# Loading the input a second time with channels on partitions, so that the first norm's units need no TensorE transposes, and reordering the first loads

## The chip, the cores and the metric

The kernel runs on one core of one Trainium2 chip. The metric is the device time of the whole kernel in microseconds (us), the median of several executions. TensorE (PE) does matrix products and transposes, VectorE (DVE) and ScalarE (ACT) elementwise work, GpSimd (POOL) a few small operations, and SyncE (SP) issues the loads.

## The reference

A two-layer decoder trunk over 256 tokens of 2048 channels, all float32. Only the start of layer 0 matters here:

```
def rms_norm(x, g):
    xf = x.astype(jnp.float32)
    y = xf * lax.rsqrt(jnp.mean(xf * xf, axis=-1, keepdims=True) + EPS)
    return (y * g.astype(jnp.float32)).astype(x.dtype)
...
    proj = hn @ w_in          # hn = rms_norm(h, even_norm), w_in: 2048 x 5392
    qa, ka, va, qkv_b, z, beta_raw, a_raw = jnp.split(proj, EVEN_SPLITS, axis=-1)
```

Behind it come a sliding-window attention and a gated delta rule, an output projection, a SwiGLU feed-forward layer, a second layer with a gated MLP mixer and another feed-forward layer, and a last norm.

## The kernel before, in words

Tokens are two tiles of 128 (t = 0, 1), channels four chunks of 512 (n = 0 to 3). A product needs its left operand with channels on partitions. That operand is a "unit": for one n and one t a tile of 128 channels x 4 x 128 tokens, in two parts, hi (rounded to the fast matmul format by ScalarE, the CAST rows) and lo (the rest, a VectorE subtraction). `fill_unit` makes it from token-major rows: four TensorE transposes into PSUM (`side<-ident,h` in the profile), a VectorE multiplication with the norm's gain (`unit<-side,gains`), then `split` for hi and lo. The other factor of the norm, one over the root mean square (`rstd`), is a number per token, and is put in only when a product's result is read from PSUM (`scale=self.rstd[t]`). It needs sums of squares: `chunk_stats` has ScalarE square each of the eight 128x512 pieces of the input (`junk<-h`) and add up; `end_norm` then has VectorE sum up and scale (`tot`, `rstda`) and GpSimd raise to the power -0.5 (`rstd<-rstda,mhalf`), once per token tile.

`dense` makes one product of 512 columns: it loads the weights in four pieces (`raw`, one for each n), splits each of a piece's four blocks into hi (`whi`, ScalarE) and lo (`wlo`, VectorE), and issues six matmuls a block: hi x hi, hi x lo and lo x hi for each token tile. The first product of the kernel is `kvg`, 272 columns wide (keys, values and gates; 96 matmuls of 128x272), the next `qa0` with 512 columns (`mm<-whi,unit ... 128x512`). `raw` has three buffers, `whi` and `wlo` six each. When kvg is done, ScalarE reads its results with `rstd` into `ba`, `unit` and `va`; the gates' small chain (`beta`, `ge`, `gg`) and the decay tables of the delta rule (`unit<-unit,gp` on VectorE, `unit<-gp,unit` on GpSimd, multiplied by `one`) run beside qa0.

The order on every engine is fixed when the kernel is built. All operations are recorded with a priority (`prio`, lower first; `schedule.early` is an earliest time in ns); a list scheduler (`plan`) with costs of its own then writes one order for all engines, and each engine keeps to it: an instruction that waits holds up all behind it. Eight completion counters are shared by SP's loads, so SP issues at most eight ahead of the oldest that has not landed.

Of the kernel before, what the change touches and what calls it, by code (L numbers as in the profile page):

```python
# [10 lines left out]
F32R = mybir.dt.float32r  # L11
BF16 = mybir.dt.bfloat16
AF = mybir.ActivationFunctionType
ALU = mybir.AluOpType
AX = mybir.AxisListType

P = 128
D = 2048
SEQ = 256
NT = SEQ // P  # L20
KB = 4
CW = 512
NCH = D // CW
# [33 lines left out]
def chunk_width(cols):  # L57
    return sum(b - a for a, b in cols)
# [256 lines left out]
class Trunk:  # L315
# [67 lines left out]

    def load_consts(self):
        nc, t = self.nc, self.t
        self.ident = self.keep((P, P), "ident")
        nc.sync.dma_start(self.ident, t["ident"])
        self.gains = self.const(t["gains"], [P, 4, 16], "gains")
        self.junk = self.keep((P, CW), "junk", BF16)
        self.mhalf = self.keep((P, 8), "mhalf")  # L390
        nc.vector.memset(self.mhalf, -0.5)
        self.phalf = self.keep((P, 8), "phalf")
        nc.vector.memset(self.phalf, 0.5)
# [57 lines left out]
    def fill_unit(self, srcs, gain=None):  # L451
# [10 lines left out]
            self.split(ps, unit[t])  # L462
        return unit


    def dense(self, w, units, off, width=CW, pcs=None, lag=0, first=False):

        nc = self.nc  # L470
        ps = [self.bank(width) for _ in range(NT)]
        pcs = range(len(units)) if pcs is None else pcs
        size = P * KB * width
        todo = deque()

        def product(t, x, k, hi, lo, st, sp):
            xh, xl = x[t]
            nc.tensor.matmul(ps[t], xh[:, k], hi, start=st, stop=False)
            nc.tensor.matmul(ps[t], xh[:, k], lo, start=False, stop=False)
            nc.tensor.matmul(ps[t], xl[:, k], hi, start=False, stop=sp)  # L480

        for unit, pc in zip(units, pcs):
            with self.prio(2 * pc - 19 if first else 0):
                raw = self.slot((P, KB, width), F32, "raw")
                o = off + pc * size
                nc.sync.dma_start(raw, w[o:o + size].rearrange("(p k n) -> p k n", p=P, k=KB))
            for k in range(KB):
                with self.prio(0):
                    tags = ("unit", "unit") if lag and k % 2 else ("whi", "wlo")
                    hi, lo = [self.slot((P, width), F32R, tag) for tag in tags]  # L490
                    nc.scalar.copy(hi, raw[:, k])
                    nc.vector.tensor_tensor(lo, raw[:, k], hi.bitcast(F32), ALU.subtract)
                with self.prio(9):
                    todo.append((unit, k, hi, lo, pc == pcs[0] and k == 0, pc == pcs[-1] and k == KB - 1))
                    product(0, *todo[-1])
                    if len(todo) > lag:
                        product(1, *todo.popleft())
        with self.prio(9):
            for x in todo:
                product(1, *x)  # L500
        return ps
# [376 lines left out]
    def even_mixer(self, gain):  # L878
        units = self.units
        off, mix, outs, c = 0, [], [], {}  # L880
        for name, cols in EVEN_CHUNKS:
            ps = self.dense(self.t["even_in"], units, off, chunk_width(cols), first=name == "kvg")
            off += D * chunk_width(cols)
            with self.prio(1):
                if name == "kvg":
                    self.end_norm()
                    ba, kk = self.gate_columns(ps), self.attn_kv(ps)
                else:
                    c[name] = self.zgate(ps) if name[0] == "z" else self.tok_tile(ps)
            if name == "kvg":  # L890
                self.schedule.early = 9000.0
                with self.prio(0):
                    self.load_tables()
                self.schedule.early = 0.0
                with self.prio(2):
                    self.gates(ba)
                    kT = self.attn_keys(kk)
            kind, i = name[:-1], int(name[-1]) if name[-1].isdigit() else 0
            with self.prio(2):
                if kind == "k":  # L900
                    keys = self.delta_k(i, c[name])
                elif kind == "q":
                    queries = self.delta_q(i, c[name])
                elif kind == "v":
                    outs.append(self.delta(i, keys, *queries, c[name]))
            with self.prio(3):
                if kind == "qa":
                    mix.append(self.new_unit())
                    for t in range(NT):
                        self.attention(i, t, c[name], mix[i][t], kT)  # L910
        w = self.t["even_out"]
        for n in range(NCH):
            self.residual(n, self.dense(w, mix, n * D * CW, pcs=range(0, 2)))
        with self.prio(1):
            rest = [self.delta_out(outs[i], c[f"z{i}"]) for i in range(2)]
        self.project(w, rest, gain, pcs=range(2, 4))
# [109 lines left out]
    def run(self):  # L1026
        g = lambda i: self.gains[:, i]
        with self.prio(-20):
            self.load_consts()
        self.begin_norm()  # L1030
        self.h = [[None] * NCH for _ in range(NT)]
        for n in range(NCH):
            with self.prio(2 * n - 20):
                self.load_hidden(n)
            with self.prio(1):
                self.units.append(self.fill_unit([self.h[t][n] for t in range(NT)], g(0)[:, KB * n:KB * (n + 1)]))
        with self.prio(1):
            for n in range(NCH):
                self.chunk_stats(n)
        self.even_mixer(g(1))  # L1040
        self.ffn(0, g(2))
        self.odd_mixer(g(3))
        self.ffn(1, None)
        with self.prio(1):
            self.finish()
# [10 lines left out]
def const_table():  # L1056
    import numpy as np

    c = np.zeros((P, NCONST, P), np.float32)
    j, i = np.meshgrid(np.arange(P), np.arange(P), indexing="ij")  # L1060
    same = (j // 64) == (i // 64)
    c[:, C_TRI] = same & (j <= i)
    c[:, C_TB] = np.where(i < 64, same & (j > i), -1.0 * (same & (j <= i)))
    c[:, C_SU] = j > i
    c[:, C_H0] = j < 64
    c[:, C_DMASK] = np.where(j <= i, 0.0, NEG)
    c[:, C_ONE] = 1.0
    c[:, C_AM] = np.where(i <= j, 0.0, NEG)
    c[:, C_AM + 1] = np.where(i > j, 0.0, NEG)
    for lv in range(2):  # L1070
        s = SB << lv
        c[:, C_LVL + lv] = (j // (2 * s) == i // (2 * s)) & ((j // s) % 2 == 0) & ((i // s) % 2 == 1)
    c[:, C_SAME] = j // SB == i // SB
    c[:, C_UP] = (j // SB == i // SB) & (j < i)
    c[:, C_DIAG] = (j % SB == i) & (i < SB)
    return c, (j == i).astype(np.float32), (j <= i).astype(np.float32)
# [14 lines left out]
def arrays_of(inputs):  # L1091
    import numpy as np

    i = {k: np.asarray(v) for k, v in inputs.items()}
    col = lambda v: v.reshape(-1, P).T
    ctab, ident, ltri = const_table()
    a = {
        "x": i["x"].reshape(NT, P, NCH, CW).transpose(0, 2, 1, 3),
        "ctab": ctab,
        "ident": ident,  # L1100
        "ltri": ltri,
        "gains": np.stack([col(i["even_norm"][0]), col(i["ffn_norm"][0]), col(i["odd_norm"][0]),
                           col(i["ffn_norm"][1])], axis=1),
        "conv": i["even_conv"][0].T.reshape(24, P, 4).transpose(1, 0, 2),
        "rows": np.concatenate([i["even_dt_bias"][0], i["even_a_log"][0], i["even_sinks"][0], i["even_onorm"][0]]),
        "bs": i["odd_b_s"][0].T,
        "ws": i["odd_w_s"][0].transpose(2, 0, 1),
        "lng": i["odd_ln_g"][0],
        "lnb": i["odd_ln_b"][0],
        "final_g": i["final_norm"],  # L1110
        "even_in": layout(i["even_w_in"][0], [c for _, c in EVEN_CHUNKS]),
        "even_out": layout(i["even_w_out"][0], PLAIN_CHUNKS),
        "odd_in": layout(i["odd_w_in"][0], ODD_CHUNKS),
        "odd_out": layout(i["odd_w_out"][0], PLAIN_CHUNKS),
    }
    for l in range(2):
        a[f"gate{l}"] = layout(i["ffn_w_gate"][l], FF_CHUNKS)
        a[f"up{l}"] = layout(i["ffn_w_up"][l], FF_CHUNKS)
        a[f"down{l}"] = layout(i["ffn_w_down"][l], PLAIN_CHUNKS)
    return {k: np.ascontiguousarray(v) for k, v in a.items()}  # L1120
# [22 lines left out]
```

## Time and profile before

| | |
|---|---|
| time, median of 3 runs (lowest, highest) | 2188.86 us (2186.94, 2188.88) |
| the profiled execution's own time | 2188.75 us |
| its span, first to last instruction | 2186.7 us |
| TensorE busy in the span | 2166.3 us (99%) |
| VectorE, ScalarE, GpSimd busy | 1326.0, 1138.5, 59.0 us |
| first matmul of kvg, first of qa0 | 10.88 us, about 26 us |

A row of the timeline gives start and length of a group of equal neighbours (xN), and in brackets how long its engine had stood idle and what ended that. Lengths are from start to full end; two neighbours overlap a little, so the distance from start to start is the smaller number.

### The profile page before, as it was taken

The page shows a single profiled execution, that of the slowest core. Times are in us where ns is not written, and L with a number is a line of the kernel's source. Part 1 is how long each engine was busy: PE and PEld are TensorE (multiplying, and loading weights), DVE is VectorE, ACT ScalarE, POOL GpSimd, SP SyncE. Part 2 cuts the span into 40 slices and gives each one's busy share as a digit, 9 for nine tenths or more (in the row PEclk, how much of TensorE's full clock was granted, in tenths as well). Part 3 has the DMA queues.
Part 4 walks back from the last instruction along what each step waited for, and adds up shares of the span by engine and source line. Part 5 has one row for each costly group of instructions (what it writes and reads, how often), then busy time and mean ns, then how long its engine had stood idle before and what let it go on. Part 6 is the DMA issues. An engine that isn't in the chain of part 4 may idle for free.

```text
span 2186.7 us, 27199 instructions
## 1 busy us (share of the span) xinstructions
PE 2166.3 (99%) x10044; PEld 1792.4 (82%) x10044; DVE 1326.0 (61%) x2265; ACT 1138.5 (52%) x2034; POOL 59.0 (3%) x68
## 2 busy tenths in 40 slices
PE   8999999999999999999999999999999999999998
PEld 7787888888888888888888888888888888888886
DVE  8796886765555555555555576665555555555553
ACT  7665654554545554444445545554555445444453
POOL 1010100000000000000010000000000000000000
PEclk9999999999999999999999999999999999999999
DMA  7342435555555555555565555555555555565553
GB/s 250 123 156 76 154 117 172 182 186 191 192 193 193 184 187 189 192 193 193 192 237 186 196 168 186 178 189 192 193 185 187 189 192 191 192 209 194 194 195 132
DMA packets 58453, 399.07 MB, mean 183 GB/s; under 512 B 6976, under 2 KB 7232, under 8 KB 11216
## 3 DMA queue, kind: packets, MB, share of 16 engines
q1 hardware_dynamic: 57168, 393.61, 53.0%
q0 software_dynamic: 1152, 3.74, 0.5%
q8 instruction: 78, 1.28, 0.2%
q14 instruction: 55, 0.45, 0.1%
HBM read 395.22 MB, written 2.10 MB: 182 GB/s over the span
## 4 chain that ended last, share of the span: by engine, by line
PE 96%; DVE 2%; ACT 1%; issue 1%; DMA 0%; POOL 0%; SPq 0%; POOLq 0%; DVEq 0%; ACTq 0%
PE mm L178 90%; PE side L178 6%; DVE unit L178 1%; DVE wlo L178 1%; ACT whi L178 0%; DMA h<-in_x 0%; ACT junk L178 0%; POOL unit L178 0%; DVE uc L178 0%; SPq L178 0%; DVE yt L178 0%; DVE h L178 0%; DVE yr L178 0%; ACT L178 0%; ACT unit L178 0%
## 5 line engine op out<-in xcount | busy, mean ns | idle before, releaser
L178 PE MATMUL mm<-whi,unit 128*128 128x512 f32 (+1 forms) x5864 | 1829.8, 391 | 0.0
L178 DVE TENSOR_TENSOR wlo<-raw,whi 128x512 fp32r<-128x512 f32 (+1 forms) x1466 | 1011.0, 691 | 806.0 <-ACT whi L178 800.7
L178 ACT CAST whi<-raw 128x512 fp32r<-128x512 f32 (+1 forms) x1466 | 909.1, 621 | 938.6 <-DVE wlo L178 752.6
L178 PEld LDWEIGHTS mm<-whi,unit 128*128 128x128 f32 x5864 | 1097.8, 188 | 226.0 <-issue 4.7
L178 PE MATMUL mm<-wlo,unit 128*128 128x512 f32 (+1 forms) x2932 | 1140.9, 390 | 0.0
L178 PEld LDWEIGHTS mm<-wlo,unit 128*128 128x128 f32 x2932 | 551.1, 188 | 110.8 <-issue 0.2
L178 PE MATMUL side<-unit,unit 128*128 128x128 f32 (+3 forms) x448 | 60.6, 285 | 0.0
L178 PEld LDWEIGHTS side<-unit,unit 128*128 128x128 f32 (+2 forms) x448 | 54.4, 182 | 5.6 <-issue 1.4
L178 ACT ACTIVATE unit<-mm,rstd 128x512 f32<-128x512 f32 (+1 forms) x84 | 56.1, 671 | 2.2
L178 PE MATMUL side<-ident,unit 128*128 128x128 f32 x356 | 55.0, 273 | 0.4 <-DVE unit L178 0.4
L178 PEld LDWEIGHTS side<-ident,unit 128*128 128x128 f32 x356 | 44.1, 140 | 12.2 <-issue 2.3
L178 DVE TENSOR_TENSOR unit<-side,unit 128x512 fp32r<-128x512 f32 (+1 forms) x64 | 43.6, 690 | 10.8 <-ACT unit L178 10.2
L178 ACT CAST unit<-side 128x512 fp32r<-128x512 f32 x60 | 35.1, 586 | 19.5 <-PE side L178 17.5
L178 DVE TENSOR_TENSOR unit<-unit,unit 128x512 fp32r<-128x512 f32 (+1 forms) x56 | 39.7, 714 | 1.0
L178 PE MATMUL mm<-unit,unit 128*128 128x512 f32 x132 | 35.9, 389 | 0.0
L178 ACT COPY unit<-side 128x512 f32<-128x512 f32 (+1 forms) x36 | 20.6, 585 | 25.4 <-PE side L178 25.4
L178 DVE SCALAR_TENSOR_TENSOR unit<-side,conv,unit 128x255 f32<-128x255 f32 (+2 forms) x72 | 31.1, 473 | 2.4 <-ACT unit L178 2.4
L178 ACT ACTIVATE junk<-h 128x512 bf16<-128x512 f32 x40 | 25.1, 628 | 11.1 <-DVE h L178 8.4
L178 DVE SCALAR_TENSOR_TENSOR unit<-mm,rstd,unit 128x512 f32<-128x512 f32 x44 | 30.9, 743 | 0.0
L178 DVE TENSOR_TENSOR h<-mm,h 128x512 f32<-128x512 f32 x40 | 25.8, 683 | 6.3 <-PE mm L178 6.3
L178 PEld LDWEIGHTS mm<-unit,unit 128*128 128x128 f32 x132 | 24.8, 188 | 5.1
L178 PE MATMUL side<-ident,h 128*128 128x128 f32 x128 | 20.7, 291 | 7.3 <-DMA h<-in_x 7.3
(119 smaller groups left out, 461.4 us busy)
## 6 DMA issues: line engine op xcount, KB each, us to landing
raw<-in_gate SPq DMA_DIRECT2D x88, 1024.0 KB, 4.8
raw<-in_up SPq DMA_DIRECT2D x88, 1024.0 KB, 4.8
raw<-in_down SPq DMA_DIRECT2D x88, 1024.0 KB, 4.9
raw<-in_even_in SPq DMA_DIRECT2D x40, 1024.0 KB, 4.9
raw<-in_odd_in SPq DMA_DIRECT2D x32, 1024.0 KB, 4.9
raw<-in_even_out SPq DMA_DIRECT2D x16, 1024.0 KB, 4.8
raw<-in_odd_out SPq DMA_DIRECT2D x16, 1024.0 KB, 4.9
raw<-in_even_in SPq DMA_DIRECT2D x4, 544.0 KB, 6.7
```

The source lines that it names most:

```text
L178: f(*map(real, args), **{k: real(a) for k, a in kw.items()})
```

## The change

The host passes the input in a second layout, `xt`: for each t and n the 128 x 4 x 128 block with channels on partitions. `first_unit` loads it straight into the buffer of a unit and multiplies with the gain in place; the transposes of the first norm are gone. The token-major input `x` is still loaded, for the sums of squares and the residual, but later and with its squares behind the units in the recorded order. The gains are asked for on ScalarE's own load queue, the identity matrix later. The first weights come second on SP's queue, ahead of the second input block.

```
-        self.ident = self.keep((P, P), "ident")
-        nc.sync.dma_start(self.ident, t["ident"])
-        self.gains = self.const(t["gains"], [P, 4, 16], "gains")
+        self.gains = self.keep((P, 4, 16), "gains")
+        nc.scalar.dma_start(self.gains, t["gains"])
+        with self.prio(-13):
+            self.ident = self.const(t["ident"], [P, P], "ident")
...
+    def first_unit(self, n, gain):
+
+        unit = []
+        for t in range(NT):
+            x = self.unit()
+            with self.prio(4 * n + 2 * t - 30):
+                self.nc.sync.dma_start(x, self.t["xt"][t, n])
+            with self.prio(1):
+                self.nc.vector.tensor_tensor(x, x, gain.unsqueeze(2).to_broadcast([P, KB, P]), ALU.mult)
+                unit.append([self.unit(F32R), self.unit(F32R)])
+                self.split(x, unit[t])
+        return unit
...
-            with self.prio(2 * pc - 19 if first else 0):
+            with self.prio(4 * pc - 29 if first else 0):
...
-                self.schedule.early = 9000.0
+                self.schedule.early = 12000.0
...
         for n in range(NCH):
-            with self.prio(2 * n - 20):
+            self.units.append(self.first_unit(n, g(0)[:, KB * n:KB * (n + 1)]))
+        for n in range(NCH):
+            self.schedule.early = 8500.0
+            with self.prio(-12):
                 self.load_hidden(n)
+            self.schedule.early = 0.0
             with self.prio(1):
-                self.units.append(self.fill_unit([self.h[t][n] for t in range(NT)], g(0)[:, KB * n:KB * (n + 1)]))
-        with self.prio(1):
-            for n in range(NCH):
                 self.chunk_stats(n)
...
+        "xt": i["x"].reshape(NT, P, NCH, KB, P).transpose(0, 2, 4, 3, 1),
```

What the scheduler makes of it is seen in the order of instructions. SP's queue at its head, before (`raw` are weights of kvg, `h` the input):

```order
L178 DMA ident_0_0_4484<-in_ident 128x128
L178 DMA gains_0_1_4486<-in_gains 128x64
L178 DMA h_0_4_4490<-in_x 128x512
L178 DMA h_0_5_4492<-in_x 128x512
L178 DMA raw_76_4494<-in_even_in 128x1088
L178 DMA h_0_20_4496<-in_x 128x512
L178 DMA h_0_21_4498<-in_x 128x512
```

and with the change, where `unit<-in_xt` is the input with channels on partitions:

```order
L178 DMA unit_4_4478<-in_xt 128x512
L178 DMA raw_52_4480<-in_even_in 128x1088
L178 DMA unit_8_4484<-in_xt 128x512
L178 DMA unit_12_4486<-in_xt 128x512
L178 DMA raw_85_4488<-in_even_in 128x1088
L178 DMA unit_16_4490<-in_xt 128x512
L178 DMA unit_20_4492<-in_xt 128x512
```

The first weights moved from fifth to second place; the eight `h` loads now stand behind the fourth piece of weights, and qa0's first weights (`raw_233`) behind those eight.

ScalarE around the end of kvg, before (`whi_200` and `unit_66` are the last casts of kvg, `whi_258` the first of qa0, `ba` reads kvg's result with `rstd`):

```order
L178 CAST whi_200_4750<-raw_175_4575 128x272
L178 CAST unit_59_4757<-unit_58_4726 128x512
L178 ACTIVATE ea_0_239_4765<-rows_0_229_4596 128x8
L178 CAST unit_66_4785<-unit_65_4754 128x512
L178 CAST whi_258_4805<-raw_257_4640 128x512
L178 CAST whi_266_4810<-raw_257_4640 128x512
L178 CAST whi_274_4817<-raw_257_4640 128x512
L178 CAST whi_282_4826<-raw_257_4640 128x512
L178 ACTIVATE ba_0_214_4834<-mm_79_4562,rstd_0_210_4789 128x2x8
```

and with the change, from kvg's last cast (`unit_34`) to qa0's first (`whi_234`):

```order
L178 CAST unit_34_4714<-unit_32_4500 128x512
L178 ACTIVATE junk_0_38_4680,ss_0_39_4684<-h_0_41_4553 128x512
L178 ACTIVATE junk_0_38_4680,ss_0_38_4679<-h_0_44_4558 128x512
L178 ACTIVATE junk_0_38_4680,ss_0_39_4684<-h_0_45_4560 128x512
L178 ACTIVATE junk_0_38_4680,ss_0_38_4679<-h_0_48_4563 128x512
L178 ACTIVATE junk_0_38_4680,ss_0_39_4684<-h_0_49_4567 128x512
L178 ACTIVATE ba_0_190_4767<-mm_55_4524,rstd_0_186_4759 128x2x8
L178 ACTIVATE unit_192_4769<-mm_55_4524,rstd_0_186_4759 128x2x64 x2
L178 ACTIVATE ba_0_190_4767<-mm_58_4539,rstd_0_189_4765 128x2x8
L178 ACTIVATE va_0_194_4773<-mm_55_4524,rstd_0_186_4759 128x128
L178 ACTIVATE unit_192_4769<-mm_58_4539,rstd_0_189_4765 128x2x64
L178 CAST whi_234_4776<-raw_233_4600 128x512
```

Before, the four casts of qa0's first weights stood ahead of the first instruction that needs `rstd`. Now five of the eight squares, and then six reads with `rstd` of both token tiles, stand between kvg's last cast and qa0's first.

VectorE at the end of kvg with the change (`unit_32` is multiplied with the gain here; then kvg's last weights, the last lo, and the sums for `rstd`):

```order
L178 TENSOR_TENSOR unit_31_4691<-unit_28_4498,unit_30_4663 128x512
L178 TENSOR_TENSOR unit_32_4500<-unit_32_4500,gains_0_0_4474 128x512
L178 TENSOR_TENSOR wlo_169_4710<-raw_151_4534,whi_168_4703 128x272
L178 TENSOR_TENSOR wlo_177_4717<-raw_151_4534,whi_176_4707 128x272
L178 TENSOR_TENSOR unit_35_4727<-unit_32_4500,unit_34_4714 128x512
L178 TENSOR_REDUCE tot_0_184_4753<-ss_0_38_4679 128x1
L178 TENSOR_SCALAR rstda_0_185_4757<-tot_0_184_4753 128x1
```

The last gain multiplication stands three instructions ahead of the last lo; before, the sums for `rstd` stood ahead of the last lo, and now behind it.

## Rows read from the trace of the kernel before

**Rows 1.** The page: span, and TensorE's busy time.

```profile
span 2186.7 us, 27199 instructions
...
PE 2166.3 (99%) x10044; PEld 1792.4 (82%) x10044; DVE 1326.0 (61%) x2265; ACT 1138.5 (52%) x2034; POOL 59.0 (3%) x68
```

**Rows 2.** Busy time by stretch: length, PE, PEld, DVE, ACT, POOL, clock, DMA.

```profile
10.80:26.00 15.20, 15.17 (x115) 14.94 (x114) 13.59 (x34) 12.82 (x35) 2.50 (x2) 1.00 1.02 373
```

**Rows 3.** Timeline of SP's queue: issue of kvg's first weights.

```profile
2.60 0.43 SPq L178 DMA_DIRECT2D raw<-in_even_in  x1
```

**Rows 4.** DMA issues at 1.6, 2.6 and 4.0 us: KB, us to landing.

```profile
h<-in_x SPq DMA_DIRECT2D x1, 256.0 KB, 2.8
...
raw<-in_even_in SPq DMA_DIRECT2D x1, 544.0 KB, 6.0
...
raw<-in_even_in SPq DMA_DIRECT2D x1, 544.0 KB, 7.2
```

**Rows 5.** VectorE by form, 0 to 23.2 us: count, busy, mean ns, idle before.

```profile
L178 DVE TENSOR_TENSOR wlo<-raw,whi 128x272 fp32r<-128x272 f32 x16 | 6.4, 436 | 1.5 <-ACT whi L178 1.4
L178 DVE TENSOR_TENSOR unit<-side,gains 128x512 f32<-128x512 f32 x8 | 5.4, 686 | 5.1 <-PE side L178 5.0
```

**Rows 6.** Timeline of VectorE in kvg.

```profile
9.08 1.50 DVE L178 TENSOR_TENSOR wlo<-raw,whi 128x272 fp32r<-128x272 f32 x4 [0.45 <-ACT whi L178]
10.50 1.47 DVE L178 TENSOR_TENSOR unit<-side,gains 128x512 f32<-128x512 f32 x2
...
15.82 1.28 DVE L178 TENSOR_TENSOR unit<-side,gains 128x512 f32<-128x512 f32 x2
```

**Rows 7.** Timeline of ScalarE, 4 to 32 us.

```profile
4.47 0.63 ACT L178 ACTIVATE junk<-h 128x512 bf16<-128x512 f32 x1 [2.45 <-DMA h<-in_x]
...
5.23 0.63 ACT L178 ACTIVATE junk<-h 128x512 bf16<-128x512 f32 x1
...
18.06 0.78 ACT L178 CAST whi<-raw 128x272 fp32r<-128x272 f32 x2
...
26.96 0.27 ACT L178 ACTIVATE ba<-mm,rstd 128x16 f32<-128x16 f32 x1 [0.48 <-POOL rstd L178]
...
27.88 2.19 ACT L178 CAST whi<-raw 128x512 fp32r<-128x512 f32 x4
...
31.84 1.28 ACT L178 ACT_TABLE_LOAD   x1
```

**Rows 8.** Timeline of GpSimd: the powers of the first norm and of another.

```profile
23.50 3.43 POOL L178 TENSOR_TENSOR rstd<-rstda,mhalf 128x1 f32<-128x1 f32 x2 [23.05 <-DVE rstda L178]
...
444.99 1.05 POOL L178 TENSOR_TENSOR rstd<-rstda,mhalf 128x1 f32<-128x1 f32 x1 [92.34 <-DVE tot L178]
447.57 0.56 POOL L178 TENSOR_TENSOR rstd<-rstda,mhalf 128x1 f32<-128x1 f32 x1 [1.53 <-DVE rstda L178]
```

**Rows 9.** Timeline of VectorE around those powers at 445 and 447.6 us.

```profile
444.94 0.69 DVE L178 TENSOR_TENSOR unit<-unit,unit 128x512 fp32r<-128x512 f32 x1
...
447.90 0.69 DVE L178 TENSOR_TENSOR wlo<-raw,whi 128x512 fp32r<-128x512 f32 x1 [0.41 <-ACT whi L178]
```

**Rows 10.** Timeline of TensorE's weight loads (PEld): two rows of transposes.

```profile
9.26 1.57 PEld L178 LDWEIGHTS side<-ident,h 128*128 128x128 f32 x8 [3.14 <-DMA h<-in_x]
...
13.32 0.48 PEld L178 LDWEIGHTS side<-ident,h 128*128 128x128 f32 x4
```

**Rows 11.** The chain that ended last: 45 matmuls of kvg in a row.

```profile
17.50 5.64 PE mm L178 x45
```

**Rows 12.** Timeline of TensorE: qa0's third matmul, a wait, the kernel's end.

```profile
26.50 0.39 PE L178 MATMUL mm<-wlo,unit 128*128 128x512 f32 x1
...
40.04 0.70 PE L178 MATMUL side<-unit,one 128*128 128x512 f32 x2 [1.25 <-DVE unit L178]
...
2176.93 0.84 PE L178 MATMUL mm<-unit,unit 128*128 128x512 f32 x3
```

**Rows 13.** Busy time by stretch at the end, columns as in rows 2.

```profile
2180.00:2181.00 1.00, 0.00 (x0) 0.00 (x0) 0.30 (x4) 0.05 (x1) 0.55 (x1) 0.75 0.00 0
```

## The prediction

> **What bounds the kernel now.** I read the page first: TensorE is busy 99% of a span of 2186.7 us [rows 1], so only about 20 us are idle, and an edit that adds no matmul work can give or take only what lies around waits. The busy time by stretch then shows where: nothing of kvg is multiplied before 10.8 us, and from 10.8 to 26.0 us TensorE is busy 15.17 of 15.20 us, VectorE 13.59, ScalarE 12.82 [rows 2]: three engines nearly full at once. The reader is to see that taking work from TensorE there does not by itself end kvg sooner. qa0's third matmul starts at 26.50 [rows 12]; with two of some 0.23 us ahead of it, qa0 starts at 26.05. That is the moment to compare: behind it TensorE works almost without a gap, so a shift of it reaches the end.
>
> **What goes.** 32 transposes. Sixteen ran before 10.8 us, in time that TensorE would have idled; the other sixteen cost 0.12 us each [rows 10], 1.9 us of the full stretch. VectorE's eight gain multiplications stay, 686 ns each [rows 5]. They read SBUF now instead of PSUM; the subtraction that reads SBUF alone takes 0.69 too [rows 9], so I take no change there.
>
> **When kvg can start.** The first `xt` block is 256 KB and SP's first load, at 0.74 us; an `h` block takes 2.8 us [rows 4], so it lands at 3.5. The gains are smaller and asked for at the same time on the other queue; were they 2 us later, nothing would move, since VectorE's second block comes much later still. SP issues a load in 0.43 us [rows 3], so kvg's first weights go out at 1.2. Before, they took 6.0 us [rows 4], though the `h` block ahead took 2.8. I take 6.0 again: 7.2. From there loads land at a steady pace: 2.60+6.0 to 4.02+7.2 is 2.6 us for 1056 KB [rows 4], 0.63 us for 256 KB. The second `xt` block lands at 7.85. Its gain stands on VectorE ahead of kvg's first four `wlo`, so these wait too, and with them TensorE behind its first one or two products, at about 7.7 instead of 10.88.
>
> **What paces kvg then.** VectorE. At 7.85 it has done one of eight gains and one of eight lo parts, and has 14 operations of 128x512 and 16 `wlo` left. An early pair takes 1.47, a later one 1.28, four `wlo` 1.50 [rows 6]: 6 x 0.74, 8 x 0.64 and 16 x 0.375, 15.5. (Neighbours overlap by some 0.04, 1.2 in all, which stands for waits for ScalarE: 1.4 before [rows 5].) The last lo part ends at 23.35; ten matmuls stand behind it, 0.125 each [rows 11]: kvg ends at 24.6, 1.45 us earlier than before. So the promise of the change is there, and small.
>
> **What stands between kvg and qa0.** The order on ScalarE now has five squares, then six reads with `rstd`, ahead of qa0's first cast; behind that cast queue VectorE's `wlo` and TensorE's whole qa0. kvg's last cast waits for the last gain, which ends about 2.05 us before the last lo (two `wlo`, the lo, and 0.6 for ScalarE's casts between): 21.3. Behind it ScalarE does two `whi` (0.36 each) and a cast (0.55), then five squares, 0.76 each start to start [rows 7], 3.8: the last ends at 26.4, token tile 0's last at 25.6. Sum and scale take VectorE some 0.2 us each: 26.0. Then GpSimd's two powers. The pair took 3.43 us here; later ones took 1.05 and 0.56 [rows 8], the first beside a VectorE operation started at 444.94, the second with VectorE idle until 447.90 [rows 9]. In the changed kernel VectorE is idle then, since its next work needs qa0's first cast. The first of the pair is the program's first power, dearer by 3.43 less two of 1.05, 1.3; so I take 0.56+1.3 and 0.56, 2.4 together, between 1.1 and 3.43. The second ends at 28.4. Three reads that need it (four took 0.92 from 26.96 to 27.88) make 0.7, the cast 0.55 [rows 7]: **qa0 starts at 29.65 instead of 26.05, +3.6 us.** Before, the squares lay beside kvg's products and the powers beside qa0's; that cover is gone, and TensorE idles from 24.6 on but for one transpose.
>
> **Behind that start.** Two things, which partly hide each other. ScalarE's order puts both loads of a function table (1.28 each [rows 7]) and some nine small operations ahead of qa0's second weights: about 6.7 us from qa0's first matmul to the fifth cast, where TensorE comes to it after 24 x 0.23 and four transposes, 5.9: 0.8 lost. And TensorE's clock: the last matmuls of the kernel start at 2176.93 [rows 12], and the granted clock is 0.75 over 2180 to 2181 [rows 13], so 2.4 GHz gave way to 1.2 GHz in it after some 2.5 us of idleness. At the start, after 3.14 us of idleness, transposes at 9.26 took 0.196 us each, those at 13.32 0.12 [rows 10]: a lower pace for up to 4.1 us. After 5 us of idleness I expect half pace again; 4.1 us of it lose 2.0, which hide the 0.8. Bounds 0.8 and 2.0; I take 1.4. On the other side TensorE's wait of 1.25 us at 40 us for VectorE's decay tables [rows 12] may shrink, since TensorE now asks five matmuls later, though the gates are later too: bounds -1.25 and 0, I take -0.7.
>
> **Sum:** 3.6 + 1.4 - 0.7 = +4.3 us on the profiled execution's 2188.75 us: **2193.0 us**. The median of the three runs is 2188.86, so the two bases agree within 0.1. 0.2%, or 4.4 us, is about what a measurement of this kernel can tell from no change; the forecast lies just inside.
>
> **At no cost:** 2 MB more to load. qa0's first weights stand behind eight `h` blocks, 6.6 MB (16.6 us at the steady pace) after the first weights: 23.8 us, and they are wanted at 29.1. Were that cover gone (reads on time), they would be the next limit, at kvg's very end.
>
> **A rule against my row.** The first weights took 6.0 us for 544 KB [rows 4]. The Trainium skill, DMA: Bandwidth & Descriptors, "Anatomy of one DMA", has about 2.0 us plus the bytes at 436 GB/s for a transfer, given for GpSimd's path. An estimate by it is 3.3 us, a landing at 4.5, and the sum would be about +2.8. The trace does not agree for this transfer (6.0) and does for an `h` block (2.6 against 2.8).
>
> **Rivals.**
> 1. *The first weights land early.* If the 6.0 us belong to a fifth place in the queue and not to this transfer, 544 KB need 2.8 plus 0.7 (288 KB more at the steady pace) and land at 4.7 us, 2.5 earlier. VectorE then waits more for the second weights, so the walk above moves by some 1.4, not 2.5. +2.9: 2191.6. For it: the `h` blocks' 2.8. Against it: the next weights' 7.2, no earlier.
> 2. *Slower beyond doubt: the powers cost what they cost.* At 3.43 for the pair qa0 starts 1.0 later: +5.3, 2194.0. It decides from 2.5 us for the pair on. For it: the only row of a first pair [rows 8]; against it, VectorE's rest.
> 3. *The change does what it seems to be for.* Reads in time and qa0 right behind kvg: -1.45, and the 1.25 wait gone: 2186.0. It needs `rstd` by 24 us, and 21.3 plus ScalarE's 5.0 forbids it unless VectorE is much faster than its rows. Even this is not faster by 0.2%.
>
> **Chances.** My forecast, with 3.2 to 5.2 as its own range, 0.42 (0.19 of it beyond 4.4); rival 1 0.22; rival 2 0.18; rival 3 0.04; what I have not seen 0.08 slower, 0.06 faster. Slower by over 0.2%: 0.19+0.18+0.08, 0.45; faster 0.06; within 0.2%: 0.49. The range goes from rival 1 with both low bounds behind the start (+1.7) to rival 2 with both high ones (+6.6): 2190.4 to 2195.4.
>
> **What would show it.** Right: kvg's first matmul at 7 to 8 us; VectorE with hardly an idle moment from there to 23; five squares in a row on ScalarE from about 22.5; TensorE idle some 5 us before the first 128x512 product at 29 to 30, ended by ScalarE; 0.45 us from matmul to matmul behind it; GpSimd's pair at 2.4. Wrong: a first landing under 5 us; the pair at 3.4 or 1.1; no gap before qa0; kvg paced by loads, VectorE idle in it; or a difference that arises behind 60 us.

## The result, and the profile after

The changed kernel takes 2192.09 us (median of 19 executions, 2191.27 to 2192.72), the kernel before 2188.8 beside it: a ratio of 1.0015, 95% interval 1.0009 to 1.0022. It is 3.3 us slower, inside the forecast's range and within 0.2%. The profiled execution took 2192.0. (The ratios below leave out two executions that took far longer, 4455.87 us in e1 and 5674.47 us in the kernel before; at e11, whose executions lie in two groups, ratio and median don't agree.)

The page (span, busy time by engine), against [rows 1]:

```profile
span 2190.2 us, 27143 instructions
...
PE 2165.3 (99%) x10012; PEld 1788.9 (82%) x10012; DVE 1327.2 (61%) x2265; ACT 1137.8 (52%) x2034; POOL 55.0 (3%) x68
```

TensorE does 32 transposes less (10012 matmuls for 10044) and the span is 3.5 us longer. So the loss is idleness or a lower pace. Where? First the loads at the head of the queue (KB, us from issue to landing), against [rows 4]:

```profile
raw<-in_even_in SPq DMA_DIRECT2D x1, 544.0 KB, 4.2
unit<-in_xt SPq DMA_DIRECT2D x1, 256.0 KB, 3.3
```

The first weights, now second in the queue, land in 4.2 us and not in 6.0. VectorE in kvg (start, length, tile; in brackets idle before and what ended it), against [rows 6]:

```profile
4.20 0.69 DVE L178 TENSOR_TENSOR unit<-unit,gains 128x512 f32<-128x512 f32 x1 [3.29 <-DMA gains<-in_gains]
...
6.19 0.69 DVE L178 TENSOR_TENSOR unit<-unit,gains 128x512 f32<-128x512 f32 x1
...
19.12 0.69 DVE L178 TENSOR_TENSOR unit<-unit,gains 128x512 f32<-128x512 f32 x1
...
20.96 0.69 DVE L178 TENSOR_TENSOR unit<-unit,unit 128x512 fp32r<-128x512 f32 x1
23.85 0.16 DVE L178 TENSOR_REDUCE tot<-ss 128x1 f32<-128x4 f32 x1 [2.19 <-ACT junk L178]
```

The second gain starts at 6.19, the last lo ends at 21.65; then VectorE waits 2.19 us for ScalarE's squares. GpSimd's powers, against [rows 8]:

```profile
24.27 0.55 POOL L178 TENSOR_TENSOR rstd<-rstda,mhalf 128x1 f32<-128x1 f32 x1 [23.83 <-DVE rstda L178]
25.03 0.55 POOL L178 TENSOR_TENSOR rstd<-rstda,mhalf 128x1 f32<-128x1 f32 x1 [0.20 <-DVE rstda L178]
```

ScalarE behind the last square (which started at 23.85 and took 0.63), against [rows 7]:

```profile
24.86 0.27 ACT L178 ACTIVATE ba<-mm,rstd 128x16 f32<-128x16 f32 x1 [0.29 <-POOL rstd L178]
...
26.28 1.66 ACT L178 CAST whi<-raw 128x512 fp32r<-128x512 f32 x3
...
30.04 1.28 ACT L178 ACT_TABLE_LOAD   x1
...
31.57 1.28 ACT L178 ACT_TABLE_LOAD   x1
...
32.98 3.21 ACT L178 CAST whi<-raw 128x512 fp32r<-128x512 f32 x6
```

TensorE; the first fence is the kernel before, where one row holds kvg's last product, at 25.91, and the first two of qa0, the second the changed kernel, against [rows 12]:

```profile
25.91 0.75 PE L178 MATMUL mm<-whi,unit 128*128 128x272 f32 x3
```

```profile
22.94 0.28 PE L178 MATMUL mm<-whi,unit 128*128 128x272 f32 x1
25.70 0.33 PE L178 MATMUL side<-ident,unit 128*128 128x128 f32 x1 [2.47 <-ACT unit L178]
26.96 0.73 PE L178 MATMUL mm<-whi,unit 128*128 128x512 f32 x2 [0.93 <-ACT whi L178]
...
28.07 0.63 PE L178 MATMUL mm<-whi,unit 128*128 128x512 f32 x1
28.50 0.63 PE L178 MATMUL mm<-wlo,unit 128*128 128x512 f32 x1
...
32.25 0.39 PE L178 MATMUL mm<-wlo,unit 128*128 128x512 f32 x1
...
34.77 0.96 PE L178 MATMUL side<-gg,unit 128*128 128x16 f32 x8
35.57 0.72 PE L178 MATMUL mm<-whi,unit 128*128 128x512 f32 x2
...
44.42 0.73 PE L178 MATMUL side<-unit,one 128*128 128x512 f32 x2 [1.74 <-DVE unit L178]
```

And the stretches (length, PE, PEld, DVE, ACT, POOL busy, granted clock, DMA):

```profile
26.00:27.00 1.00, 0.07 (x2) 0.04 (x1) 0.06 (x1) 1.00 (x4) 0.00 (x0) 1.00 1.02 426
...
28.00:29.00 1.00, 1.00 (x4) 0.73 (x3) 1.00 (x3) 1.00 (x4) 0.00 (x0) 0.50 0.97 410
...
32.00:33.00 1.00, 1.00 (x6) 0.81 (x5) 0.57 (x4) 0.99 (x3) 0.00 (x0) 1.00 1.05 442
```

kvg's last product starts at 22.94, so kvg ends 2.97 us earlier than before. Then TensorE idles 3.4 us but for one transpose (2.47 + 0.93), and qa0 starts at 26.96, 0.92 later than before. Its products then come 0.43 us apart (28.07, 28.50): the granted clock is 0.50, 1.2 GHz, from 28 us on and 1.00, 2.4 GHz, again from 32 on. At 44.42 stands the wait for the decay tables, 1.74 us where it was 1.25.

What makes the tables late is seen on VectorE: `gg` is the result of the gates' chain, and `gp` its two parts, a cast on ScalarE and then the VectorE row shown here, from which the tables are made. The kernel before, then the changed one:

```profile
33.59 0.17 DVE L178 TENSOR_TENSOR gg<-gg,ea 128x16 f32<-128x16 f32 x1
...
34.51 0.17 DVE L178 TENSOR_TENSOR gp<-gg,gp 128x16 fp32r<-128x16 f32 x1
```

```profile
33.31 0.18 DVE L178 TENSOR_TENSOR gg<-gg,ea 128x16 f32<-128x16 f32 x1
...
38.76 0.17 DVE L178 TENSOR_TENSOR gp<-gg,gp 128x16 fp32r<-128x16 f32 x1
```

The gates are done 0.3 us earlier than before, but `gp` comes 4.25 us later: six casts of qa0's weights now stand ahead of its cast on ScalarE (the last row of ScalarE above), seven `wlo` ahead of it on VectorE. From `gp` to TensorE's first table product it is 5.5 us before and 5.7 now.

I counted products in both traces. qa0's 49th starts at 41.16 us, before at 38.40 (+2.76, with the same side work behind it but for one transpose); k0's first at 56.54, before 52.66 (+3.88); the kernel's 1001st at 338.61, before 335.07 (+3.54), and the span is 3.5 longer. So all of the loss arises before 57 us.

### The profile page after: what moved, and what is told of

It reads as the page before. It is cut to its first block, busy times and chain, and to the rows that moved or that the text cites. A ratio compares the mean times of both kernels' runs of the same rounds, so it can differ in the third digit from the quotient of the medians.

```text
span 2190.2 us, 27143 instructions
## 1 busy us (share of the span) xinstructions
PE 2165.3 (99%) x10012; PEld 1788.9 (82%) x10012; DVE 1327.2 (61%) x2265; ACT 1137.8 (52%) x2034; POOL 55.0 (3%) x68
## 4 chain that ended last, share of the span: by engine, by line
PE 96%; DVE 2%; ACT 1%; issue 1%; POOL 0%; DMA 0%; POOLq 0%; DVEq 0%; ACTq 0%
PE mm L178 90%; PE side L178 6%; DVE unit L178 1%; DVE wlo L178 1%; ACT junk L178 0%; ACT whi L178 0%; DMA gains<-in_gains 0%; ACT unit L178 0%; DVE uc L178 0%; POOL unit L178 0%; DVE yt L178 0%; DVE h L178 0%; POOL rstd L178 0%; DVE yr L178 0%; POOLq L1154 0%
## 5 line engine op out<-in xcount | busy, mean ns | idle before, releaser
L178 PEld LDWEIGHTS side<-ident,unit 128*128 128x128 f32 x356 | 44.4, 141 | 15.9 <-ACT unit L178 2.7
L178 DVE SCALAR_TENSOR_TENSOR unit<-side,conv,unit 128x254 f32<-128x254 f32 (+2 forms) x72 | 31.3, 474 | 2.5 <-ACT unit L178 2.5
L178 DVE SCALAR_TENSOR_TENSOR unit<-mm,rstd,unit 128x512 f32<-128x512 f32 x44 | 30.9, 744 | 0.0
L178 ACT CAST unit<-unit 128x512 fp32r<-128x512 f32 x32 | 19.8, 619 | 11.8 <-DVE unit L178 11.6
(120 smaller groups left out, 447.6 us busy)
```

Source lines behind the costliest of these rows:

```text
L178: f(*map(real, args), **{k: real(a) for k, a in kw.items()})
```

## The experiments

| run | median us | over the kernel before beside it | ratio (95%) | qa0 starts | TensorE's longest waits behind it, us |
|---|---|---|---|---|---|
| changed kernel | 2192.09 | 3.3 | 1.0015 (1.0009 to 1.0022) | 26.96 | 1.74 at 44.4 |
| e1 spare products | 2191.61 | 3.2 | 1.0015 (1.0007 to 1.0024) | 27.00 | 2.01 at 43.6 |
| e2 decay later | 2192.62 | 4.2 | 1.0017 (1.0009 to 1.0026) | 26.36 | 2.17 at 115.1 |
| e3 both | 2190.90 | 2.5 | 1.0011 (1.0003 to 1.0020) | 26.83 | 2.17 at 114.5 |
| e4 casts first | 2190.34 | 2.0 | 1.0007 (0.9998 to 1.0015) | 24.95 | 1.60 at 42.8 |
| e5 `ea` early | 2191.05 | 2.5 | 1.0012 (1.0003 to 1.0021) | 26.95 | 0.82 at 44.4 |
| e6 casts, gates | 2188.68 | 0.2 | 1.0002 (0.9993 to 1.0011) | 24.94 | 1.70 at 43.4 |
| e7 VectorE busy | 2193.22 (one execution) | 4.7 | | 27.60 | 1.75 at 45.7 |
| e8 before, load order | 2188.12 | -0.4 | 0.9998 (0.9990 to 1.0007) | 24.97 | 1.76 at 39.7 |
| e9 lo on VectorE | 2195.31 | 6.6 | 1.0031 (1.0019 to 1.0043) | 27.21 | 2.41 at 62.8 |
| e10 e6 + lo on VectorE | 2193.91 | 5.2 | 1.0025 (1.0015 to 1.0036) | 24.84 | 2.37 at 58.3 |
| e11 e8 + lo on VectorE | 2193.20 | 4.5 | 1.0012 (1.0004 to 1.0021) | 24.43 | 2.17 at 58.9 |
| e12 e10, squares behind | 2192.87 | 4.1 | 1.0021 (1.0012 to 1.0031) | 23.43 | 1.47 at 30.9, 2.85 at 60.6 |

The third column is the difference of two medians taken on one chip (before: 2188.8 for the change, 2188.38 for e1 to e4, 2188.51 for e5 to e8, 2188.75 for e9 to e12); the intervals of the ratios reach 1.4 to 2.6 us to each side, so a difference under some 2.5 us between two runs is not shown by the times. What is said below of smaller ones rests on the traces, each of one execution. Most edits below give an operation an earliest time (`schedule.early`, ns), so that the list scheduler places it later.

**e1 to e3: the lower pace, and the wait at 44 us.** Theory A: the loss behind qa0's start is TensorE's pace. Theory B: it is the order on ScalarE, which makes the gates and the decay tables late. e1 fills the idleness with spare work, e2 moves the products that read the tables, e3 does both.

```
             if name == "kvg":
+                self.schedule.early = 22100.0
+                with self.prio(9):
+                    spare = self.side(P, CW)
+                    for i in range(16):
+                        nc.tensor.matmul(spare, units[3][0][0][:, i % 4], units[3][1][0].rearrange("p k n -> p (k n)"),
+                                         start=(i == 0), stop=(i == 15))
```

```
             rep = self.side(P, 4, P)
+            self.schedule.early = 47000.0
             for i in range(2):
                 nc.tensor.matmul(rep.rearrange("p h i -> p (h i)"), self.one,
                                  tg[i].rearrange("p h i -> p (h i)"), start=(i == 0), stop=(i == 1))
+            self.schedule.early = 0.0
```

> The changed kernel with 16 spare 128x512 products between kvg and qa0, into a bank that nothing reads, so that TensorE hardly idles there (before: 3.9 us). Theory A, the lower pace behind that idleness is the loss: qa0's 25th product moves from 35.57 to about 33.5 us and the whole gets 2.0 us faster, 2190.1. Theory B, the decay tables set a fixed time: qa0's 25th product comes as early, but TensorE's wait for VectorE's unit still ends at 44.4, grows from 1.74 to about 3.8 us, and the time stays 2192.1.

> The changed kernel with the products that read the decay tables moved from the 150th to the 183rd product's place on TensorE, so that their tables are there in time. Both theories: the wait of 1.74 us at 44.4 goes and the time falls by 1.7, to 2190.4. If the delay only comes back at a later wait: 2192.1.

> Both edits together. Theory A: the two add, 2.0 + 1.7, 2188.4, each worth as much as alone. Theory B: also 3.7 less, 2188.4, but the spare products alone were worth 0 then. If neither, 2192.

TensorE in e1, timeline and one stretch of it:

```profile
23.10 2.92 PE L178 MATMUL side<-unit,unit 128*128 128x512 f32 x12
...
27.00 0.73 PE L178 MATMUL mm<-whi,unit 128*128 128x512 f32 x2
...
33.00 0.39 PE L178 MATMUL mm<-whi,unit 128*128 128x512 f32 x1
33.59 1.06 PE L178 MATMUL side<-gg,unit 128*128 128x16 f32 x8 [0.20 <-DVE gg L178]
34.50 0.71 PE L178 MATMUL mm<-whi,unit 128*128 128x512 f32 x2
```

```profile
28.00:29.00 1.00, 1.00 (x6) 0.78 (x6) 1.00 (x3) 1.00 (x4) 0.00 (x0) 1.00 0.98 401
```

With no idleness the clock stays at 1.00 and qa0's first 24 products with their three transposes take 6.2 us (27.00 to 33.23), in the changed kernel 7.8 (26.96 to 34.77). So the lower pace costs 1.6 us there. But 0.4 are lost at once: TensorE now waits for `gg` (33.23 to 33.59). At 43.6 the next wait is 0.3 longer. Of the 2.0 us forecast 0.8 are left in the span (2189.4) and 0.1 in the comparison of medians. Theory A has the mechanism and not the price; B's fixed 44.4 us is wrong too, since the tables came 0.8 earlier: VectorE's `wlo` between them wait for TensorE in their turn.

e2 has no wait at 44 us, and gained nothing. TensorE in e2 (timeline, then a stretch behind it):

```profile
115.10 0.50 PE L178 MATMUL side<-unit,same 128*128 128x512 f32 x1 [2.17 <-POOL unit L178]
```

```profile
116.00:118.00 2.00, 2.00 (x7) 1.54 (x5) 0.34 (x1) 1.03 (x3) 0.20 (x1) 0.50 0.00 0
```

A wait of 2.17 us for GpSimd stands at 115 us instead, where the changed kernel has none, and the clock went to 0.50 behind it as well. That this is the same delay come back is argued: the scheduler placed much of what lies between anew. In e3 the same 2.17 at 114.5 was followed by a clock of 1.00. Together the edits are worth 0.8 us by the medians, not 3.7.

**e4 to e6: the order on ScalarE.** e4 puts qa0's casts ahead of the reads; e5 puts `ea` beside the other exponentials, so that one table load fewer stands ahead of the fifth cast; e6 does both, with the gates ahead of weights. The first fence is e4's edit; of the second, e5 has the lines on `ea` alone; e6 has both fences.

```
                 if name == "kvg":
                     self.end_norm()
+                    self.schedule.early = 24100.0
                     ba, kk = self.gate_columns(ps), self.attn_kv(ps)
+                    self.schedule.early = 0.0
```

```
         nc.scalar.activation(beta, ba[:, 0], AF.Exp, scale=-1.0)
+        ea = self.small([P, B_H], "ea")
+        nc.scalar.activation(ea, self.alog, AF.Exp)
+        nc.vector.tensor_scalar(ea, ea, -1.0, None, ALU.mult)
...
-        ea = self.small([P, B_H], "ea")
-        nc.scalar.activation(ea, self.alog, AF.Exp)
-        nc.vector.tensor_scalar(ea, ea, -1.0, None, ALU.mult)
...
+                with self.prio(-1):
+                    self.gates(ba)
                 with self.prio(2):
-                    self.gates(ba)
```

> The changed kernel with the reads of kvg's result recorded for a later time, so that qa0's first four casts stand ahead of them on ScalarE. Theory A: qa0 starts right behind the last square, at about 25.2 instead of 26.96; idleness before it 2.2 instead of 3.9 us; 1.7 us less, 2190.4, and 2188.4 if the clock holds too. Theory B: the gates come up to 2.4 us later, the wait for the decay tables takes all of it, 2192 to 2193.

> The changed kernel with ea (the exponential of the rows) put beside the other exponentials, ahead of the logarithm, so that one table load of 1.28 us instead of two stands ahead of qa0's second weights. Theory A, TensorE's lower pace is the loss: at that pace TensorE comes to the fifth cast too late to gain from it, 0 to 0.3 us less, 2191.9. Theory B, the order on ScalarE behind qa0's start is the loss: gates and fifth cast 1.4 us earlier, the wait of 1.74 us at 44.4 shrinks by as much, 2190.7.

> The casts of qa0 ahead of the reads (as in e4, which was 1.75 us faster than the change), ea beside the other exponentials, and the gates recorded with a higher priority than weights, so that their parts are cast ahead of qa0's third weights. Theory B: the wait of 1.6 us for the decay tables goes or halves, 2188.6 to 2189.5, no slower than before. Theory C, VectorE is nearly full from 100 to 150 us (46.9 of 50 us) and gives the gain back there, as in e2 at 112 us: 2190.3.

TensorE's waits in e4 (first fence), in e5 (second) and in e6 (third):

```profile
24.95 0.73 PE L178 MATMUL mm<-whi,unit 128*128 128x512 f32 x2 [1.91 <-ACT whi L178]
...
42.81 0.72 PE L178 MATMUL side<-unit,one 128*128 128x512 f32 x2 [1.60 <-DVE unit L178]
```

```profile
44.36 0.73 PE L178 MATMUL side<-unit,one 128*128 128x512 f32 x2 [0.82 <-DVE unit L178]
```

```profile
24.94 0.73 PE L178 MATMUL mm<-whi,unit 128*128 128x512 f32 x2 [1.91 <-ACT whi L178]
...
43.43 0.73 PE L178 MATMUL side<-unit,one 128*128 128x512 f32 x2 [1.70 <-DVE unit L178]
```

The granted clock behind that start, in e4 and in e6:

```profile
28.00:29.00 1.00, 1.00 (x8) 0.74 (x6) 0.00 (x0) 0.97 (x6) 0.00 (x0) 1.00 1.03 434
```

```profile
28.00:32.00 4.00, 4.00 (x15) 3.20 (x14) 1.12 (x4) 3.97 (x10) 0.00 (x0) 0.74 0.98 387
```

e4: qa0 2.0 us earlier, the clock held, and 1.3 us of time, where theory A had 3.7 with the clock held and B none.

e5: 0.8. The wait went from 1.74 to 0.82, but not as theory B has it: the tables come no earlier, 44.36 for 44.42. TensorE came later, since its clock stood at 0.50 from 26 to 33 us and not from 28 to 31 (the last product ahead of the wait starts at 43.15, in the changed kernel at 42.29). The fifth cast came 1.5 us earlier (31.45 for 32.98) and `gp` 1.9 (36.87 for 38.76), and then four `wlo` beside GpSimd's products took VectorE 5.90 us. What e5 gains stands behind: the second pair of table products starts at 52.66 and not at 53.12.

e6: 3.1 us less than the change, nearly the whole loss, and as fast as before within the interval. The time was forecast, but not its reason: the wait is 1.70 still, though `gp` comes at 33.67. Its executions lie in two groups, 7 at 2188.0 to 2188.7 and 4 at 2190.1 to 2190.8, with a mean granted clock of 0.999 and of 0.998; the profiled one is of the latter (2190.09) and shows the clock at 0.74 over 28 to 32, where e4 after the same 1.91 us of idleness shows 1.00. e6 loads the 2 MB more as the change does, so most of the loss is the order behind kvg, and not these loads. Which share each of e6's three edits has is not separated.

**e7: what makes a power dear.** Three spare subtractions on VectorE behind the sums:

```
                     self.end_norm()
+                    self.schedule.early = 22700.0
+                    spare = self.unit()
+                    for i in range(3):
+                        self.nc.vector.tensor_tensor(spare, units[3][0][0].bitcast(F32), units[3][0][1].bitcast(F32), ALU.subtract)
+                    self.schedule.early = 0.0
```

> The changed kernel with three spare 128x512 subtractions on VectorE behind the sums for rstd, so that GpSimd's second power runs beside them. If a busy VectorE makes a power dear: first power 0.55, second 1.0 to 2.4 us, qa0 0.5 to 1.8 us later. If only the kernel's first power is dear, or neither: 0.55 each. The time 2192 to 2194.

GpSimd in e7, and in e8, where the pair runs beside VectorE's `wlo`:

```profile
24.53 0.56 POOL L178 TENSOR_TENSOR rstd<-rstda,mhalf 128x1 f32<-128x1 f32 x1 [24.08 <-DVE rstda L178]
25.28 0.93 POOL L178 TENSOR_TENSOR rstd<-rstda,mhalf 128x1 f32<-128x1 f32 x1 [0.20 <-DVE rstda L178]
```

```profile
22.37 4.20 POOL L178 TENSOR_TENSOR rstd<-rstda,mhalf 128x1 f32<-128x1 f32 x2 [21.92 <-DVE rstda L178]
```

The second power, which ran beside the subtractions, took 0.93, just under the 1.0 expected, and the first, with VectorE idle, 0.56; from kvg's last product to qa0's first it is 4.4 us, 0.4 more than in the change. No power is dear for being the kernel's first (0.55 at 24.27 in the changed kernel); a busy VectorE makes it dearer, by 0.4 us here. Beside a run of `wlo` the pair took 4.20 in e8 and 3.43 in [rows 8], 1.2 to 1.6 more for each; that this is the same cause is argued, since no run took VectorE's work away there.

**e8: one part of the change alone.** The kernel before, with its first weights behind the first input block and the gains on ScalarE's queue; the transposes stay.

```
-        self.gains = self.const(t["gains"], [P, 4, 16], "gains")
+        self.gains = self.keep((P, 4, 16), "gains")
+        nc.scalar.dma_start(self.gains, t["gains"])
...
-            self.nc.sync.dma_start(hx, self.t["x"][t, n])
+            with self.prio(2 * n + t - 20):
+                self.nc.sync.dma_start(hx, self.t["x"][t, n])
...
-            with self.prio(2 * pc - 19 if first else 0):
+            with self.prio(2 * pc - 19.5 if first else 0):
```

> The kernel before with one part of the change alone: first weights asked for right behind the first input block, gains on ScalarE's queue; transposes and all else stay. If the weights' 6.0 us were their place in the queue: they land about 4.2 us after they are asked for, as in the changed kernel. If they belong to 544 KB: 6.0 again. In both cases the input blocks come later, which the transposes wait for, and kvg's end is not earlier: 2188.4 to 2189.5.

DMA issues in e8 at 1.65 us:

```profile
raw<-in_even_in SPq DMA_DIRECT2D x1, 544.0 KB, 4.5
```

In third place the weights land in 4.5 us: the 6.0 of [rows 4] belonged to their place in the queue and not to 544 KB. I was wrong about kvg: it starts at 8.43 instead of 10.88 and qa0 at 24.97, 1.07 earlier, as early as in e6. Yet the time is the same as before within its interval. The wait for the decay tables grew from 1.25 to 1.76 us. This kernel keeps the transposes, and it starts qa0 as early and is as fast as e6 (2188.12 and 2188.68): no run shows a gain of the second input layout beyond what the order of the loads gives.

**e9 to e12: the decay tables themselves.** VectorE's first three 128x128 products of a table took 2.98 us in the changed kernel, where others take 0.2 each, while GpSimd makes the lo tables. Theory D: put these on VectorE too, and the tables are in time. Theory C: VectorE gives it back later.

```
-            nc.gpsimd.tensor_tensor(lo, self.bc(self.gparts[1][:, t, hs].bitcast(F32)),
+            nc.vector.tensor_tensor(lo, self.bc(self.gparts[1][:, t, hs].bitcast(F32)),
```

and for e12 also

```
+            self.schedule.early = 24050.0 if n == 3 else 0.0
             with self.prio(1):
                 self.chunk_stats(n)
```

> The changed kernel with the lo products of the decay tables (four 128x512 on GpSimd) moved to VectorE. Theory D, VectorE and GpSimd slow each other there (three 128x128 products took VectorE 2.98 us, others 0.2 each): four more operations of 0.69 us on VectorE, but the tables come some 2 us earlier, the wait of 1.74 us goes, 2190.4. Theory B, the tables are late because the gates are late: the wait stays over 1 us, 2191.5 or more.

> e6 (2188.7) with the same move. Theory D: its wait of 1.70 us goes, 2187.0, under the kernel before. Theory C, VectorE's load gives it back between 100 and 150 us: 2188.7.

> e8 (the kernel before with the first weights behind the first input block, 2188.1) with the same move: theory D 2186.4, its wait of 1.76 us gone; theory C 2188.1. Says whether the input on partitions is worth anything once the order behind kvg is mended: e10 against this one.

> e10 with the last two of the eight squares recorded for a time behind qa0's first casts. qa0's first weights land at 23.1 us, so qa0 starts at about 23.7 instead of 24.95, after 0.7 us of idleness, too little for the lower pace: 1.2 us less than e10 (2185.8 by theory D). If the later rstd makes the decay tables late again, the wait takes it back: 2187 to 2188.5.

VectorE's first three table products in the changed kernel, and in e9:

```profile
40.59 2.98 DVE L178 TENSOR_SCALAR unit<-unit,gp 128x128 fp32r<-128x128 f32 x3
```

```profile
41.08 0.67 DVE L178 TENSOR_SCALAR unit<-unit,gp 128x128 fp32r<-128x128 f32 x3
```

TensorE's waits in e9 and in e12:

```profile
62.75 2.15 PE L178 MATMUL side<-unit,unit 64*128 64x128 f32 x16 [2.41 <-DVE unit L178]
```

```profile
23.43 0.73 PE L178 MATMUL mm<-whi,unit 128*128 128x512 f32 x2 [0.39 <-ACT whi L178]
...
30.90 1.28 PE L178 MATMUL side<-gg,unit 128*128 128x16 f32 x8 [1.47 <-DVE gg L178]
...
60.58 1.68 PE L178 MATMUL side<-unit,unit 64*128 64x128 f32 x16 [2.85 <-DVE unit L178]
```

The slowdown was real: without GpSimd the same three take 0.67 us, and no wait of note is left at 44. But no kernel became faster, and the medians rose: e9 by 3.3 us against the change, e10 by 5.0 against e6, e11 by 4.9 against e8 (3.1 by its ratio). TensorE waits at 58 to 63 us instead, 2.2 to 2.9 us, at the first scores of the attention; in e9 and e10 the clock is 0.50 over 64 to 66 and 60 to 64 us behind it, in e12 0.58 over 62 to 64.

VectorE has four more operations (2.8 us) ahead of those scores. In all four kernels it also stands still four or five times for 0.38 us just ahead of them, waiting for ScalarE, which waits for VectorE in its turn (0.35 each time). That these make the scores late is argued from the order and not shown. Theory D falls. Of theory C the loss is seen, at 60 us and not at 100 to 150; its cause, VectorE's load, is as little shown.

The stretch behind e11's wait of 2.17 us at 58.9:

```profile
60.00:62.00 2.00, 2.00 (x23) 2.00 (x22) 2.00 (x6) 0.16 (x1) 0.00 (x0) 1.00 0.00 0
```

e11 shows how much of the loss hangs on the clock. Its executions lie in two groups, 2188.1 to 2189.2 (4, the profiled one among them), with a mean granted clock of 0.999, and 2191.3 to 2194.1 (7), with 0.996 to 0.997. The profiled one has the wait of 2.17 us at 58.9 and a clock of 1.00 behind it, and is as fast as e8: there the move only put a wait of 1.76 us at 40 in the place of one of 2.17 at 59. Where the clock of the seven fell no profile shows. e10 against e11, which was to say whether the input on partitions is worth anything, shows no gain of it: 2193.91 and 2193.20.

e12 starts qa0 at 23.43, 2.6 us earlier than before. This is lost ahead of the tables: 1.47 us of wait for the gates at 30.9 and a clock of 0.50 over 32 to 34, so that qa0's 49th product starts at 39.45, before at 38.40. In the end e12 is 1.1 us under e10, about the 1.2 forecast, though not clear of noise. That it is 4.1 us slower than the kernel before is for the most part the move, as in e10.

## Why the prediction was right

The size came out nearly right by luck: qa0 started 2.7 us earlier than forecast, and what came behind that start cost 2.6 us where 0.7 was forecast.

- *kvg's first matmul at 7.7 us*: 5.92. The failed step is "I take 6.0 again" for the first weights' landing; it was 4.2, by the place in the queue (4.5 in e8). That is rival 1's mechanism, and its +2.9 is nearer to the +3.3 than my +4.3, by the same luck: by its sum too qa0 starts some 2.2 us later. The Trainium skill, DMA: Bandwidth & Descriptors, "Anatomy of one DMA", gave an estimate of 3.3 us for this transfer, nearer to 4.2 than my row was.
- *VectorE paces kvg, 15.5 us from the second block*: right, 15.46 (6.19 to 21.65); only its start was 1.7 early. It was set by the first block: the gains landed at 4.1, and VectorE went from that block's gain (4.20) and lo part to the second gain without standing still but for 0.7 us. So "were they 2 us later, nothing would move" does not hold with loads that land this early.
- *Five squares and the reads stand ahead of qa0's first cast*: right. 5.1 us were forecast from the last gain's end to the last square's end, 4.8 measured (19.81 to 24.57, where the last square's sum has been read).
- *The pair of powers at 2.4*: failed. "The first of the pair is the program's first power, dearer by 1.3" is wrong; each took 0.55, the first still beside a square, and from the last square's end to the second `rstd` there were 1.0 us, not 2.0. e7 shows that a busy VectorE makes a power dearer, which I had half seen in [rows 9]; in the changed kernel VectorE was all but idle. Rival 2 falls with it. The Trainium skill, SBUF — State Buffer, "Who interferes with whom", has a VectorE instruction with two SBUF inputs contend with a GpSimd one that reads SBUF; 0.56 against 0.93 in e7 agrees.
- *qa0 starts 3.6 us later*: 0.92. Of the 2.7 between, 1.5 are the earlier start, as it reached VectorE's last gain, 0.3 the stretch from there through the squares, and 1.0 the powers, less 0.1 for the reads.
- *1.4 behind that start (0.8 to 2.0)*: 1.84 by qa0's 49th product (2.76 less 0.92). Right in kind: the half pace (0.43 from product to product, granted clock 0.50 from 28 to 31 us) and the table loads hide each other in part, 0.4 of 1.6 in e1. The 4.1 us of lower pace at the kernel's start [rows 10] were no measure of it: the granted clock there is 1.00, in each us from 9 to 14, and what slowed those transposes stays open.
- *0.7 back from the wait at 40 us*: failed, it grew by 0.5. The failed step is "bounds -1.25 and 0", by which the wait could not grow: the gates came 0.3 earlier, but `gp` behind them 4.25 later, by the weights' casts and `wlo` ahead of it, and TensorE only 3.9 later. Taking out the second table load did not bring the tables earlier (e5). Together with a new wait of 0.25 at 53 us and small pieces, 1.1 more were lost up to k0's first product.

Sum: 0.92 + 1.84 + 1.12 = 3.9 at k0's first product, 3.5 at the end of the span; 0.4 come back behind k0, in pieces that I did not follow. Rival 3 needed `rstd` by 24 us and got it at 25.6; e4, e6 and e8 show that even qa0 1.1 us earlier than before is not a faster kernel.

**Where the gain went.** kvg ends 2.97 us earlier, twice the 1.45 forecast. ScalarE's order turned it into idleness, and the idleness into a lower clock. With that order mended (e6) qa0 starts 1.1 us earlier than before, but the wait for the decay tables is 1.70 instead of 1.25, and in four of eleven executions the clock falls. Where that wait is taken away by more work for VectorE (e10, e12), another of 2.4 to 2.9 us stands at 58 to 61 us. In none of these runs does the chain on VectorE and GpSimd follow what TensorE gains at 23 us. Which operation of VectorE would have to go or move to let a gain through was not found.

## What to carry to other kernels

Ahead of a change that lets one engine start earlier, follow the in-order queues of the others through the next two or three waits: here what was won at 23 us was asked for again at 27, 31, 44 or 60 us. When work loses its cover (squares beside products), its cost appears whole, and the idleness can be paid for a second time in the clock (1.6 us in e1's comparison). A wait that gets shorter is no proof that what it waits for came earlier: look at the moment at which it ends (e5). Take the price of an operation from a row with the same neighbours, above all for VectorE and GpSimd.

## What the runs showed of the hardware

- A power of 128x1 on GpSimd took 0.55 us with VectorE idle, 0.93 beside subtractions with two SBUF inputs, and a pair beside a run of them 3.43 and 4.20. The other way, VectorE's 128x128 products took 1.0 us each beside GpSimd's 128x512 products and 0.22 without.
- After 3.4 to 3.7 us of idleness but for one transpose TensorE's granted clock went to 0.50 in every profile that had it (the change, e2, e5, e7, e9). After 1.5 to 2.9 us it went down in some (e6 at 25 us, e12 at 31 and 61, e10 at 58, e9 at 63, e2 at 115) and not in others (e4 and e10 at 25, e1 at 44, e11 at 59, e3 at 114): 1.91 us in e4 and e6, 2.17 us in e2 and e3, each with both outcomes. One kernel can have both: the two groups of executions of e6 and of e11, 1.7 and 5 us apart, differ in their mean granted clock (0.999 and 0.998, 0.999 and 0.996 to 0.997).
- A load of 544 KB landed 4.2, 4.5 and 6.0 us after its issue in second, third and fifth place of a queue that had just started.
